# Layer 1 on sums and differences of mirrored tokens, with Fourier weights folded over mirrored channels

## The chip, the cores and the metric

The kernel runs on one core of one Trainium2 chip. The metric is the device time of one execution in microseconds; it is taken from repeated runs, and from one further run that a hardware profiler recorded.

## What is computed

Two layers act on 512 tokens of 2048 features, all in fp32. Cut to what matters here:

```python
for l in range(2):
    shift, scale, gate = split(silu(c) @ w_ada[l] + b_ada[l], 3)
    h = layernorm(x) * (1 + scale) + shift
    u_f, z_f, cq, ckv, k_r, z_a = split(h @ w_in[l])     # 1024, 1024, 512, 256, 64, 1024 columns
    f = real(fft over tokens and over the 128 channels of each of 8 groups of u_f)
    y_f = (f @ w_fmix[l] per group) * silu(z_f)
    y_a = attention(rmsnorm(cq) @ w_q_b, rmsnorm(ckv) @ w_kv_b, k_r) * silu(z_a)
    y = concat(y_f, y_a) @ w_out[l]
    x = layernorm(ALPHA * x + gate * y, ln_g[l], ln_b[l])
```

The real part of a Fourier transform over tokens n and channels m is a sum of cos·cos and −sin·sin products. The cosine in n takes only the sum of the tokens n and 512 − n, the sine only their difference; the same holds for the channels m and 128 − m.

## The kernel before

**Products.** Each fp32 matrix is split into a high part with fewer bits and the rest, and a product is three matmuls (`mm3`, L143 to L146): high·high, high·low, low·high. `split` (L139) makes the parts: ScalarE copies the high one, VectorE subtracts to get the low one. The host sorts the tokens so that n and 512 − n lie in the same row of the blocks 0 and 2, or 1 and 3, of 128 tokens.

**Weights.** `Stream` holds the units of weights in the order of use. A `dense` unit is 256 rows by 512 columns: one DMA from SP's queue into one of three raw buffers (`wr`), one `split`. `st = Stream(4, 2)` loads four units ahead of use and splits two ahead. Converted weights, the activations `h` (16 tiles) and most results share a pool of 35 buffers of 4 KB a partition (`b`). Another pool of nine (`t`) holds short-lived tiles of 512 columns, six buffers (`ada`) take tiles of `w_ada`, and two (`acc`) their running sums. Matmuls write to eight PSUM banks: four `pa` for groups of columns, four `pm` for the rest.

**Order.** The code is unrolled; a planner places each engine's instructions by their place in the text, and may take a later one where an earlier one waits and buffers are free. At run time each engine keeps that order.

**Layer 1.** While the output projection of layer 0 ends row block by row block (L1048), `half_h` (L538) already builds `h` for the tokens of blocks 0 and 1: transposes on TensorE, scale and shift on ScalarE, `split`. `first_group` (L568) takes the first 512 Fourier columns (UA): five units for half of the tokens, then the other half, then `fourier_weights(1)` (two products of fp32 matrices per half of the groups), then three units for all tokens. It is followed by UB, by two groups of Fourier gate columns (ZF), by CQ, CKV and by two groups of attention gate columns (ZA). A group of 512 columns is 8 units of 24 matmuls, each 512 wide. `tm_group` puts tokens on PSUM's partitions, `fm_group` features. `folded` (L627) adds and subtracts the two halves of the tokens of UA and UB, and `fourier` (L597) runs beside the next groups: per block of 128 channels, 14 products with the table over tokens and 6 with the channel table times `w_fmix`. `silu` reads a gate group straight from PSUM; the attention gates wait in DRAM (`szd`).

**Modulation.** `bg_step(n)` (L304) emits n tiles of `w_ada` at a time, each a 512 KB DMA and scaled additions on VectorE (one of 1024 columns per tile for the gates). Layer 1's last 32 tiles, for its output gate, are emitted at 0.7 tiles per unit (`G1`) from UB on, on POOL's DMA queue. `finish` (L245) sums an accumulator over the partitions with transposes and a reduction, adds the bias, and after the last columns writes the gate to DRAM (`gated`). All of it is drained before attention starts.

**Output projection.** Four groups of 512 columns (L1019); for each, the gate's part is read from `gated`, spread over the partitions, into `gb`, and `residual` (L994) multiplies a bank by it and adds it to the scaled input. This frees the bank for the next group.

Of the kernel before, what the change touches and what calls it, by code (L numbers as in the profile page):

```python
# [18 lines left out]
P = 128  # L19
# [4 lines left out]
H = 8  # L24
# [14 lines left out]
class Unit:  # L39
    """One piece of a weight: loaded as it is, then split into a high and a low part."""  # L40
# [15 lines left out]
class Stream:  # L56
    """The weights in the order of their use; next() also starts those that follow."""

    def __init__(self, ahead_raw, ahead):
        self.units, self.ar, self.ac, self.pos = [], ahead_raw, ahead, 0  # L60
        self.limit = None

# [17 lines left out]
def trunk_kernel(ctx: ExitStack, tc: tile.TileContext, x, c, positions, w_ada, b_ada, w_in, q_norm,  # L80
                 w_q_b, kv_norm, w_kv_b, w_fmix, w_out, ln_g, ln_b, dft, chan, invf, odds, out):
    nc = tc.nc
    # layer 0: blocks of 128 features of the input per step, and the part of a step over which the modulation of the
    # next one is spread
    SZ = [1, 2, 3, 4, 6]
    LEADS = [0.5, 0.6, 0.7, 0.5, 0.5]
    # tiles of w_ada per half unit of weights: ahead of need, last step, attention, output projection, layer 1
    ZP, ZL, AP, CP, G1 = 0.5, 1.0, 1.0, 1.4, 0.7
    # half units between the end of a sum over tiles and its sum over the partitions (DL0: in the first step); half
    # units of layer 1 without w_ada tiles  # L90
    DL0, DLY, LATE1 = 2, 3, 4
# [100 lines left out]
    szd = drp.tile([H, P, S], F32, name="szd")  # L192
    gated = drp.tile([DEPTH, D], F32, name="gated")

# [32 lines left out]
    def ada(l, pieces, cols, tiles=None):  # L227
        """One 512 KB tile of w_ada[l] per step; pieces: the column ranges."""
# [38 lines left out]
    def finish_late(steps=None):  # L267
        """Sums over the partitions, some steps after their last term so that TensorE does not wait."""
# [54 lines left out]
    def normalise(t, sums=None):  # L323
        """t: two [128, 1024] tiles, -> (t - mean) * rstd, in place. sums: of the rows of the two tiles, if known."""
# [39 lines left out]
    def dense(src, row0, col0, n, nr=2):  # L364
# [9 lines left out]
        return Unit(load, conv)  # L374
# [52 lines left out]
    for l in range(DEPTH):  # L427
# [7 lines left out]
        else:  # L435
            add_groups(w_in[l], [UA, UB] + ZF + [CQ, CKV] + ZA[:1])
# [10 lines left out]
    def tm_half(banks, w, act, k0, n, first, last, tbs=range(NT)):  # L447
        """token-major: out[tokens, n] += act[k, tokens]^T w[k, n]"""
# [9 lines left out]
    def fm_half(banks, w, act, k0, first, last):  # L458
        """feature-major: out[features, tokens] += w[k, features]^T act[k, tokens]"""
# [9 lines left out]
    def fourier_weights(l):  # L469
# [18 lines left out]
        return cw, dt  # L488

# [48 lines left out]
    def half_h(half, k):  # L538
        """The blocks k, k + 1 of layer 1's features, for half of the tokens."""
        ps = pm()  # L540
        t = t2([P, S])
        ts = slice(half * 256, half * 256 + 256)
        for i in range(2):
            for tb in (2 * half, 2 * half + 1):
                o = i * 256 + (tb % 2) * P
                PE.transpose(out=ps[:, o:o + P], in_=xh[tb][k // 8][:, ((k + i) % 8) * P:][:, :P], identity=ident)  # L546
        for i in range(2):
            m, o = k + i, slice(i * 256, i * 256 + 256)
            if half == 0:
                h[m] = big([P, 2, S])  # L550
            A.activation(t[:, o], ps[:, o], AF.Identity, scale=modT[1][:, 16 + m:17 + m], bias=modT[1][:, m:m + 1])  # L551
            split(h[m][:, 0, ts], h[m][:, 1, ts], t[:, o])
# [3 lines left out]
    for l in range(DEPTH):  # L556
        sums = {}

        def tm_group(g, work=lambda: None):
            banks = [pa() for _ in range(NT)]  # L560
            for k2 in range(8):
                tm_half(banks, st.next(), h, k2 * 2, g[1], k2 == 0, k2 == 7)
                bg_step(G1)
# [4 lines left out]
        def first_group():  # L568
            """The first group of layer 1: half of the tokens starts while the others' layer norm runs."""
            nonlocal cw, dt  # L570
            banks = [pa() for _ in range(NT)]
            for k2 in range(NE):
                tm_half(banks, early[k2], h, k2 * 2, 512, k2 == 0, False, (0, 1))
            for k2 in range(NE, 8):
                half_h(0, k2 * 2)
            for k2 in range(8):
                half_h(1, k2 * 2)
                if k2 < NE:
                    tm_half(banks, early[k2], h, k2 * 2, 512, k2 == 0, False, (2, 3))
            cw, dt = fourier_weights(1)  # L580
# [4 lines left out]
        def fm_group(work=lambda: None):  # L585
            banks = [pa() for _ in range(4)]
            for k2 in range(8):
                fm_half(banks, st.next(), h, k2 * 2, k2 == 0, k2 == 7)
                bg_step(G1)
# [51 lines left out]
        def runner(gen):  # L641
            return lambda: next(gen, None)
# [17 lines left out]
        def latent(src, n, nt):  # L660
            if l == 0:
                p = src
            else:
                t = [big([P, 2, nt], F32) for _ in range(2)]
                p = [t[tb // 2][:, tb % 2] for tb in range(NT)]
                for tb in range(NT):
                    A.copy(p[tb], src[tb][:, :nt])
# [5 lines left out]
            rsqrt_eps(rstd, ssq, 4, 'rms', 1.0 / n)  # L673
            for tb in range(NT):
                V.tensor_scalar(p[tb][:, :n], p[tb][:, :n], rstd[:, tb:tb + 1], None, op0=ALU.mult)
# [10 lines left out]
        def rotary_key(p):  # L686
# [11 lines left out]
            split(kb[:, 0, :, 0], kb[:, 1, :, 0], kr)  # L698
# [166 lines left out]
        if l == 0:  # L865
            # the modulation arrives with the weights: some of the features at a time
# [79 lines left out]
        else:  # L946
            fa = fourier(0, folded(first_group()))
            ub = tm_group(UB, runner(fa))
            drain(fa)
            fb = fourier(1, folded(ub))  # L950
            gate_f(0, silu(fm_group(runner(fb))))
            zs = silu(fm_group(runner(fb)))
            drain(fb)
            gate_f(1, zs)
            lq = latent_q(tm_group(CQ))
            next(lq)
            lkv = latent_kv(tm_group(CKV, runner(lq)))
            next(lkv)
            spill(0, silu(fm_group(runner(lkv))))
            rq = rotary_queries(1)  # L960
            next(rq)
            spill(1, silu(fm_group(runner(rq))))
        project(0)
        drain(rq)
        if l == 1:
            drain(bg)
            finish_late()
# [32 lines left out]
        def finish_rows(tb):  # L1000
# [15 lines left out]
            if l == 0:  # L1016
                normalise(rt[tb], sums if tb < NT - 1 else None)
# [102 lines left out]
```

## Time and profile before

| | us |
|---|---|
| median of three runs (lowest, highest) | 1429.96 (1428.58, 1431.32) |
| profiled execution, first to last instruction | 1430.3 |
| TensorE busy | 1383.3 |
| VectorE busy | 985.8 |
| ScalarE busy | 531.7 |

No time is listed for the profiled execution apart from its span, which is 0.3 us above the median of the runs. A matmul's recorded time includes its way through the array, which overlaps the next one: the distance between starts is what a stream of them costs.

### The profile page before, as it was taken

The page shows a single profiled execution, that of the slowest core. Times are in us where ns is not written, and L with a number is a line of the kernel's source. Part 1 is how long each engine was busy: PE and PEld are TensorE (multiplying, and loading weights), DVE is VectorE, ACT ScalarE, POOL GpSimd, SP SyncE. Part 2 cuts the span into 40 slices and gives each one's busy share as a digit, 9 for nine tenths or more (in the row PEclk, how much of TensorE's full clock was granted, in tenths as well). Part 3 has the DMA queues.
Part 4 walks back from the last instruction along what each step waited for, and adds up shares of the span by engine and source line. Part 5 has one row for each costly group of instructions (what it writes and reads, how often), then busy time and mean ns, then how long its engine had stood idle before and what let it go on. Part 6 is the DMA issues. An engine that isn't in the chain of part 4 may idle for free. (4 is left out here: it accounts for less than half of the span.)

```text
span 1430.3 us, 18410 instructions
## 1 busy us (share of the span) xinstructions
PE 1383.3 (97%) x6941; PEld 1165.0 (81%) x6941; DVE 985.8 (69%) x1598; ACT 531.7 (37%) x931; POOL 50.9 (4%) x77
## 2 busy tenths in 40 slices
PE   4899999999999999999989999999999999999996
PEld 3688888787888888788877888888988888888885
DVE  7799999848968998666689942422325587833448
ACT  6713331224546554212176232422324565522110
POOL 1000000000000000000133100000000000000001
PEclk9999999999999999999999999999999999999999
DMA  8888898824753337876268922520352322272312
GB/s 276 294 286 280 271 348 286 303 74 133 220 192 119 118 104 246 295 253 236 102 234 309 330 71 83 154 70 21 116 148 81 97 59 67 65 252 89 103 60 117
DMA packets 134288, 249.02 MB, mean 174 GB/s; under 512 B 19053, under 2 KB 49913, under 8 KB 134201
## 3 DMA queue, kind: packets, MB, share of 16 engines
q1 hardware_dynamic: 127160, 224.53, 48.4%
q0 software_dynamic: 7040, 23.34, 4.6%
q8 instruction: 54, 0.88, 0.3%
q14 instruction: 34, 0.27, 0.1%
HBM read 235.23 MB, written 12.60 MB: 173 GB/s over the span
## 5 line engine op out<-in xcount | busy, mean ns | idle before, releaser
L144 PE MATMUL pa<-b,b 128*128 128x512 f32 (+2 forms) x1456 | 559.5, 385 | 6.5 <-ACT b L140 5.6
L146 PE MATMUL pa<-b,b 128*128 128x512 f32 (+2 forms) x1456 | 554.8, 382 | 2.3 <-DVE b L141 2.3
L145 PE MATMUL pa<-b,b 128*128 128x512 f32 (+2 forms) x1456 | 555.3, 382 | 0.0
L141 DVE TENSOR_TENSOR b<-wr,b 128x1024 fp32r<-128x1024 f32 (+2 forms) x200 | 228.0, 1148 | 233.2 <-PE pa L145 117.9
L140 ACT CAST b<-wr 128x1024 fp32r<-128x1024 f32 (+2 forms) x200 | 197.7, 998 | 391.5 <-PE pa L146 207.9
L144 PEld LDWEIGHTS pa<-b,b 128*128 128x128 f32 x1456 | 275.0, 189 | 58.8 <-ACT b L140 6.7
L146 PEld LDWEIGHTS pa<-b,b 128*128 128x128 f32 x1456 | 275.1, 189 | 54.2 <-DVE b L141 3.2
L145 PEld LDWEIGHTS pa<-b,b 128*128 128x128 f32 x1456 | 274.9, 189 | 48.7 <-issue 0.7
L240 DVE SCALAR_TENSOR_TENSOR acc<-ada,cact,acc 128x1024 f32<-128x1024 f32 (+2 forms) x193 | 227.7, 1185 | 13.3 <-DMA ada<-in_w_ada_dram 11.3
L144 PE MATMUL pm<-b,b 128*128 128x512 f32 (+3 forms) x592 | 201.7, 343 | 1.8 <-ACT b L140 0.8
L145 PE MATMUL pm<-b,b 128*128 128x512 f32 (+3 forms) x592 | 196.7, 333 | 0.0
L146 PE MATMUL pm<-b,b 128*128 128x512 f32 (+3 forms) x592 | 196.2, 332 | 0.0
L144 PEld LDWEIGHTS pm<-b,b 128*128 128x128 f32 x592 | 111.3, 189 | 19.0 <-ACT b L140 2.7
L145 PEld LDWEIGHTS pm<-b,b 128*128 128x128 f32 x592 | 111.9, 189 | 11.4 <-DVE b L141 0.2
L146 PEld LDWEIGHTS pm<-b,b 128*128 128x128 f32 x592 | 111.8, 189 | 10.5
L140 ACT CAST b<-pm 128x512 fp32r<-128x512 f32 (+1 forms) x116 | 58.1, 533 | 100.3 <-PE pm L605 43.8
L141 DVE TENSOR_TENSOR b<-pm,b 128x512 fp32r<-128x512 f32 (+1 forms) x116 | 68.4, 611 | 34.8 <-ACT b L140 34.7
L140 ACT CAST b<-t 128x512 fp32r<-128x512 f32 (+1 forms) x82 | 41.2, 537 | 53.3 <-DVE t L856 25.6
L900 DVE TENSOR_TENSOR b<-b,pm 128x512 f32<-128x512 f32 (+1 forms) x88 | 55.4, 656 | 5.2 <-PE pm L146 5.0
L141 DVE TENSOR_TENSOR b<-t,b 128x512 fp32r<-128x512 f32 (+1 forms) x82 | 45.2, 576 | 4.0 <-ACT b L140 2.9
L822 ACT ACTIVATE t<-pa,mx 128x512 f32<-128x512 f32 x64 | 43.9, 693 | 10.5 <-DVE mx L819 10.5
L819 DVE TENSOR_REDUCE mx<-pa 128x1 f32<-128x512 f32 x64 | 42.3, 685 | 2.4 <-PE pa L817 2.0
(138 smaller groups left out, 941.8 us busy)
## 6 DMA issues: line engine op xcount, KB each, us to landing
wr<-in_w_in_dram SPq DMA_DIRECT2D x105, 512.0 KB, 4.6
ada<-in_w_ada_dram SPq DMA_DIRECT2D x96, 512.0 KB, 5.5
wr<-in_w_out_dram SPq DMA_DIRECT2D x64, 512.0 KB, 4.1
ada<-in_w_ada_dram SPq DMA_DIRECT2D x96, 256.0 KB, 4.7
ada<-in_w_ada_dram POOLq DMA_DIRECT2D x32, 512.0 KB, 6.1
b<-in_x_dram SPq DMA_DIRECT2D x16, 512.0 KB, 6.5
ada<-in_w_ada_dram SPq DMA_DIRECT2D x32, 192.0 KB, 5.1
wr<-in_w_q_b_dram SPq DMA_DIRECT2D x48, 128.0 KB, 2.9
```

Source lines behind the costliest of these rows:

```text
L140: A.copy(hi, src)
L141: V.tensor_tensor(lo, src, f(hi), op=ALU.subtract)
L144: PE.matmul(o, lh, rh, start=first, stop=False)
L145: PE.matmul(o, lh, rl, start=False, stop=False)
L146: PE.matmul(o, ll, rh, start=False, stop=last)
L240: V.scalar_tensor_tensor(out=a, in0=t[:, r - r0], scalar=cact[:, r:r + 1], in1=a, op0=ALU.mult, op1=ALU.add)
L819: V.reduce_max(mx, ps, axis=AX.X, negate=True)
L822: A.activation(e, ps, AF.Exp, bias=mx, accum_out=ssum)
L900: V.tensor_tensor(s_[tb], s_[tb], banks[tb][:, :n], op=ALU.add)
```

## The change

Layer 1's `h` is built as sums (first 256 columns) and differences (last 256) of mirrored tokens; every projection of layer 1 works on these. The gate groups and the latents add and subtract the halves again after their product (`unfolded`, `latent`), with a factor of one half. All four gate groups now go to DRAM and come back. The Fourier columns are folded over mirrored channels when they are converted: 520 sums (64 per group and the eight middle channels) and 504 differences. The sums of tokens meet only the sums of channels, the differences only the differences (`u_pass`). The tokens 0 and 256, each its own mirror, share a row; its difference over the folded channels is summed on VectorE (`xacc`). Order: ZA0, ZF0, Fourier weights, U, ZF1 (beside the Fourier transform), CQ, CKV, ZA1. The last 32 tiles of `w_ada` are emitted with ZF0, CKV, ZA1 and the first group of the output projection, and are drained after that group.

```diff
-    ZP, ZL, AP, CP, G1 = 0.5, 1.0, 1.0, 1.4, 0.7
+    ZP, ZL, AP, CP, G0, G1 = 0.5, 1.0, 1.0, 1.4, 0.7, 1.2
+    ROWS = [0, 2, 1, 3]
+    FW, UAH = 2, 6
...
+    def fold_unit(src, k):
...
+            w, hi, lo = big([P, 1024], F32), big([P, 1024]), big([P, 1024])
+            c = t.rearrange("p (g c) -> p g c", c=P)
+            e = w[:, 0:512].rearrange("p (g c) -> p g c", c=64)
+            V.tensor_tensor(e[:, :, 1:64], c[:, :, 1:64], c[:, :, 127:64:-1], op=ALU.add)
+            V.tensor_tensor(w[:, 520:1024].rearrange("p (g c) -> p g c", c=63), c[:, :, 1:64], c[:, :, 127:64:-1],
+                            op=ALU.subtract)
+            A.copy(e[:, :, 0], c[:, :, 0])
+            A.copy(w[:, 512:520], c[:, :, 64])
+            split(hi, lo, w)
...
+                V.scalar_tensor_tensor(out=xacc[0][:, :520], in0=w[:, :520], scalar=r, in1=xacc[0][:, :520],
+                                       op0=ALU.mult, op1=ALU.add)
...
+    def pair_h(p, k):
...
+        V.tensor_tensor(v[:, :, 0], t[:, :, 0], t[:, :, 1], op=ALU.add)
+        V.tensor_tensor(v[:, :, 1], t[:, :, 0], t[:, :, 1], op=ALU.subtract)
...
+            def part(w, k0, p, last):
+                wh, wl = w
+                for j in range(4):
+                    js = slice(j * P, (j + 1) * P)
+                    o = banks[j].rearrange("p (x b t) -> p x b t", x=2, b=2)[:, :, p]
...
+                        mm3(o, wh[:, i, js], wl[:, i, js], ah, al, p == 0 and k0 + i == 0, last and i == 1)
+
             for k2 in range(NE):
-                tm_half(banks, early[k2], h, k2 * 2, 512, k2 == 0, False, (0, 1))
+                part(early[k2], k2 * 2, 0, False)
...
             for k2 in range(NE, 8):
-                tm_half(banks, st.next(), h, k2 * 2, 512, False, k2 == 7)
+                fm_half(banks, st.next(), h, k2 * 2, False, k2 == 7)
...
+        def u_pass():
+
+            e, o, b = [pa(), pa()], [pa(), pa()], [pm(), pm()]
+            for k in range(NK):
+                wh, wl = st.next()
+                for p in range(2):
+                    es, os_ = slice(p * P, p * P + P), slice(256 + p * P, 256 + p * P + P)
+                    for bank, ts, cs in ((e[p], es, slice(256, 520)), (b[p], es, slice(0, 256)),
+                                         (o[p], os_, slice(520, 1024))):
+                        mm3(bank[:, :cs.stop - cs.start], h[k][:, 0, ts], h[k][:, 1, ts], wh[:, cs], wl[:, cs],
+                            k == 0, k == NK - 1)
...
+        def fourier_folded(u):
...
+            for b in range(4):
...
+                for i in range(2):
...
+                    mm3(pp[:, 0:258], c[:, 0, gs], c[:, 1, gs], at[:, 0, 0:258], at[:, 1, 0:258], True, False)
+                    mm3(pp[:, 0:258], n[:, 0, gs], n[:, 1, gs], an[:, 0, 0:258], an[:, 1, 0:258], False, True)
+                    mm3(pq[:, 0:256], s_[:, 0, gs], s_[:, 1, gs], at[:, 0, 256:512], at[:, 1, 256:512], True, True)
...
+        def unfolded(banks, dst):
+
+            for j in range(4):
+                t, z = t2([P, S]), t2([P, S])
+                A.copy(t, banks[j])
+                V.tensor_tensor(z[:, 0:256], t[:, 0:256], t[:, 256:512], op=ALU.add)
+                V.tensor_tensor(z[:, 256:512], t[:, 0:256], t[:, 256:512], op=ALU.subtract)
+                A.activation(z, z, AF.Silu, scale=0.5)
+                SP.dma_start(szd[dst + j], z)
...
+            unfolded(first_group(), 0)
+            st.ahead(4, UAH)
+            unfolded(fm_group(ada=G0), H)
+            cw, nq, dt = folded_constants(1)
+            st.ahead(4, 2)
+            fb = fourier_folded(u_pass())
+            unfolded(fm_group(runner(fb, FW)), H + 4)
...
+                if l == 1 and g == 0:
+                    drain(bg)
+                    finish_late()
+                    SP.dma_start(gb, gated[l:l + 1, gs].broadcast_to([P, 512]))
                 for tb in range(NT):
                     residual(g, tb, banks[tb], gb)
```

## Rows read from the trace of the kernel before

**Rows 1.** The page, part 1: busy us (share of the span) and instructions of each engine.

```profile
PE 1383.3 (97%) x6941; PEld 1165.0 (81%) x6941; DVE 985.8 (69%) x1598; ACT 531.7 (37%) x931; POOL 50.9 (4%) x77
```

**Rows 2.** Waits of TensorE, whole span: us in total, times, longest us.

```profile
PE pm L350 <- ACT b L345: 8.9, 4, 2.7
PE pa L144 <- ACT b L140: 5.6, 3, 2.2
```

**Rows 3.** Windows of layer 1: length, busy us of each engine, clock, DMA.

```profile
780.00:800.00 20.00, 20.00 (x92) 16.34 (x91) 19.48 (x26) 9.80 (x17) 5.84 (x11) 1.00 0.96 351
...
820.00:840.00 20.00, 20.00 (x100) 16.71 (x98) 6.20 (x12) 2.92 (x5) 0.00 (x0) 1.00 0.37 122
...
860.00:900.00 40.00, 40.00 (x200) 33.57 (x199) 13.16 (x22) 11.28 (x18) 0.00 (x0) 1.00 0.26 76
```

**Rows 4.** Timeline of TensorE, products 512 wide: start us, us, instruction.

```profile
1147.00 0.39 PE L144 MATMUL pa<-b,b 128*128 128x512 f32 x1
...
1151.76 0.39 PE L144 MATMUL pa<-b,b 128*128 128x512 f32 x1
```

**Rows 5.** Timeline of TensorE, products 256 wide.

```profile
1141.50 0.28 PE L145 MATMUL pa<-b,b 128*128 128x256 f32 x1
...
1144.13 0.28 PE L146 MATMUL pa<-b,b 128*128 128x256 f32 x1
```

**Rows 6.** Timeline of TensorE: a Fourier block of 14 products, and what follows.

```profile
798.22 0.28 PE L144 MATMUL pm<-b,b 128*128 128x258 f32 x1
...
800.27 0.39 PE L146 MATMUL pa<-b,b 128*128 128x512 f32 x1
```

**Rows 7.** Timeline of TensorE: the fp32 products of the Fourier weights, and what follows.

```profile
776.07 3.05 PE L478 MATMUL pm<-b,b 128*128 128x512 f32 x6
778.56 0.80 PE L144 MATMUL pa<-b,b 128*128 128x512 f32 x1
```

**Rows 8.** The page, part 5: out<-in xcount | busy, mean ns | idle before.

```profile
L144 PEld LDWEIGHTS pa<-b,b 128*128 128x128 f32 x1456 | 275.0, 189 | 58.8 <-ACT b L140 6.7
```

**Rows 9.** Groups of VectorE by line and shape.

```profile
L141 DVE TENSOR_TENSOR b<-wr,b 128x1024 fp32r<-128x1024 f32 x169 | 205.5, 1223 | 187.8 <-PE pa L145 109.1 <-ACT b L140 50.9 <-issue 14.8
...
L240 DVE SCALAR_TENSOR_TENSOR acc<-ada,cact,acc 128x1024 f32<-128x1024 f32 x150 | 192.4, 1283 | 5.4 <-DMA ada<-in_w_ada_dram 3.6
...
L240 DVE SCALAR_TENSOR_TENSOR acc<-ada,cact,acc 128x512 f32<-128x512 f32 x28 | 20.2, 751 | 3.5 <-DMA ada<-in_w_ada_dram 3.3
...
L141 DVE TENSOR_TENSOR b<-t,b 128x256 fp32r<-128x256 f32 x34 | 13.0, 418 | 0.7 <-PE pm L681 0.5 <-ACT b L140 0.2
...
L634 DVE TENSOR_TENSOR t<-pa,t 128x512 f32<-128x512 f32 x6 | 4.1, 684 | 0.6 <-ACT t L633 0.6
```

**Rows 10.** Windows at the border of the layers.

```profile
737.40:741.00 3.60, 3.59 (x9) 2.87 (x10) 3.14 (x6) 3.60 (x8) 2.57 (x3) 0.54 1.00 312
...
751.00:754.50 3.50, 2.03 (x9) 0.84 (x7) 3.50 (x6) 3.50 (x10) 0.73 (x1) 0.98 1.04 414
754.50:758.00 3.50, 3.50 (x9) 2.59 (x10) 3.04 (x12) 2.09 (x4) 0.66 (x1) 0.53 0.60 221
...
758.00:763.00 5.00, 5.00 (x33) 4.29 (x32) 4.78 (x8) 4.62 (x11) 1.63 (x3) 1.00 0.55 165
```

**Rows 11.** Timeline, all engines: from the sums of the last gate columns to their store.

```profile
1116.71 1.03 PE L253 MATMUL pm<-ident,acc 128*128 128x128 f32 x8
...
1119.57 0.33 SPq L262 DMA_DIRECT2D gated<-t  x1
```

**Rows 12.** DMA issues: count, KB each, median us to landing.

```profile
t<-gated SPq DMA_DIRECT2D x8, 256.0 KB, 4.6
...
gated<-t SPq DMA_DIRECT2D x2, 8.0 KB, 3.0
```

**Rows 13.** Timeline of VectorE: the residual of a group in the output projection.

```profile
1284.09 0.70 DVE L996 TENSOR_TENSOR pa<-pa,t 128x512 f32<-128x512 f32 x1 [0.30 <-PE pa L146]
1284.83 0.69 DVE L997 SCALAR_TENSOR_TENSOR b<-b,pa 128x512 f32<-128x512 f32 x1
```

More of the change, by code (lines that the diff above doesn't have):

```diff
@@ L61, in __init__, with ahead @@
         self.limit = None
+    def ahead(self, raw, conv):
+        self.ar, self.ac = raw, conv
     def add(self, u):
@@ L435, in trunk_kernel @@
         else:
[L436 removed]
+            add_groups(w_in[l], [ZA[0], ZF[0]])
+            for k in range(NK):
+                st.add(fold_unit(w_in[l], k))
+            add_groups(w_in[l], [ZF[1], CQ, CKV])
             for k2 in range(8):
@@ L488, in fourier_weights, with folded_constants, keep @@
         return cw, dt
+    def folded_constants(l):
+        def keep(shape, dt=F32R):
+            n[0] += 1
+            if n[0] <= 6:
+                return adp.tile(shape, dt, tag="ada", name=nm("fc"))
+            return big(shape, dt)
+        n = [0]
+        cw, nq, dt = [[None, None], [None, None]], [], []
+        cc = big([P, 2, P], F32)
+        GP.dma_start(cc, chan.rearrange("a p c -> p a c"))
+        wf = big([P, G, P], F32)
+        SP.dma_start(wf, w_fmix[l].rearrange("g m d -> m g d"))
+        for hf in range(2):
+            for a in range(3):
+                lhs = big([P, P], F32)
+                if a < 2:
+                    for d in range(2):
+                        V.tensor_copy(lhs[:, d * 64:d * 64 + 64], cc[:, a, 0:64])
+                else:
+                    V.tensor_copy(lhs, cc[:, 0, 64:65].broadcast_to([P, P]))
+                ps = pm()
+                PE.matmul(ps, lhs, wf[:, hf * 4:hf * 4 + 4].rearrange("p g d -> p (g d)"), start=True, stop=True)
+                t = keep([P, 2, 512])
+                if a < 2:
+                    V.memset(f(t), 0.0)
+                    for d in range(2):
+                        rs = slice(d * 64, d * 64 + 64)
+                        o, i = (x.rearrange("p (g e c) -> p g e c", e=2, c=P)[:, :, d] for x in (t[rs, 0], ps[rs]))
+                        A.copy(o, i)
+                        V.tensor_tensor(t[rs, 1].rearrange("p (g e c) -> p g e c", e=2, c=P)[:, :, d], i, f(o),
+                                        op=ALU.subtract)
+                    cw[a][hf] = t
+                else:
+                    for g in range(4):
+                        cs, m = slice(g * P, g * P + P), ident[:, 120 + hf * 4 + g:121 + hf * 4 + g]
+                        scaled(t[:, 0, cs], t[:, 1, cs], ps[:, cs], m)
+                    nq.append(t)
+        for k in range(2):
+            t = keep([P, 2, S])
+            for a in range(2):
+                GP.dma_start(t[:, a], dft[a, k * P:(k + 1) * P, :])
+            dt.append(t)
+        return cw, nq, dt
     def rotary_tables():
@@ L557, in trunk_kernel, with tm_group @@
         sums = {}
-        def tm_group(g, work=lambda: None):
+        def tm_group(g, work=lambda: None, ada=0):
             banks = [pa() for _ in range(NT)]
@@ new lines, in gates @@
+        def gates():
+            for j in range(8):
+                sz = t2([P, S])
+                SP.dma_start(sz, szd[H + j])
+                yj = yf[j // 2][:, j % 2]
+                V.tensor_tensor(yj, yj, sz, op=ALU.mult)
+                yield
+        def unfolded(banks, dst):
[6 more added lines that the diff above has]
+                SP.dma_start(szd[dst + j], z)
@@ L644, in drain, with runner, run @@
+        def runner(gen, n=1):
+            def run():
+                for _ in range(n):
+                    next(gen, None)
+            return run
         def drain(gen):
@@ L664, in latent @@
                 t = [big([P, 2, nt], F32) for _ in range(2)]
-                p = [t[tb // 2][:, tb % 2] for tb in range(NT)]
-                for tb in range(NT):
-                    A.copy(p[tb], src[tb][:, :nt])
+                p = [t[tb % 2][:, tb // 2] for tb in range(NT)]
+                for tb in range(2):
+                    b = t2([P, S])
+                    A.copy(b[:, :nt], src[tb + 2][:, :nt])
+                    V.tensor_tensor(p[tb], src[tb][:, :nt], b[:, :nt], op=ALU.add)
+                    V.tensor_tensor(p[tb + 2], src[tb][:, :nt], b[:, :nt], op=ALU.subtract)
+            half = 0.5 if l else 1.0
             ssq = sm(4, 'ssq')
@@ L697, in rotary_key @@
             kb = big([P, 2, NT, 2, 64])
-            split(kb[:, 0, :, 0], kb[:, 1, :, 0], kr)
+            if l == 0:
+                split(kb[:, 0, :, 0], kb[:, 1, :, 0], kr)
+            else:
+                scaled(kb[:, 0, :, 0], kb[:, 1, :, 0], kr, 0.5)
             for a in range(2):
@@ L1016, in finish_rows @@
             if l == 0:
-                normalise(rt[tb], sums if tb < NT - 1 else None)
+                normalise(rt[tb], sums if tb != ROWS[-1] else None)
         for g in range(4):
@@ L1048, in trunk_kernel @@
                         SP.dma_start(lgb[i][j], src[l:l + 1, j * 1024:(j + 1) * 1024].broadcast_to([P, 1024]))
-                for tb in range(NT):
+                for tb in ROWS if l == 0 else range(NT):
                     ts = slice(tb * P, (tb + 1) * P)
@@ L1056, in trunk_kernel @@
                     finish_rows(tb)
-                    if l == 0 and tb == HA:
+                    if l == 0 and tb == ROWS[HA]:
                         xh = rt
```

163 lines of the change are left out of this document (120 added, 43 removed).

## The prediction, made before the changed kernel ran

> **What bounds the kernel now.** I read the page's first part, the waits of TensorE, the windows of layer 1 and then the timeline of each place that the change touches. TensorE is busy in 1383.3 of 1430.3 us, VectorE in 985.8, ScalarE in 531.7 [rows 1]. After the first loads the waits of TensorE are few: 8.9 us where the first rows are normalised, 5.6 us on weights or activations from ScalarE, none longer than 2.7 us [rows 2]. So a TensorE product that goes away shortens the run, unless what fed it beside comes late. In layer 1's windows TensorE is busy throughout, while VectorE goes from 19.5 of 20 us at 780 to 800 (it runs ahead with the tiles of w_ada there) down to 6.2 of 20 and 13.2 of 40 later [rows 3]. The border of the layers is the one weak place: at 751 to 754.5 TensorE is busy 2.0 of 3.5 us, and in the next 3.5 us the granted clock is 0.53, its 1.2 GHz level [rows 10].
>
> **The price of a product.** From start to start: 21 products 512 wide from 1147.00 to 1151.76 are 0.227 us each [rows 4]; 22 products 256 wide from 1141.50 to 1144.13 are 0.120 us each [rows 5]. The cost follows the width, and the weight load (189 ns recorded [rows 8]) hides even behind 0.120 us.
>
> **TensorE's sum.** (a) U before: two groups of 8 units of 24 products, 384 × 0.227 = 87.1 us. After: 16 units, each 2 halves × 3 banks × 3 products of 264, 256 and 504 columns, so 96 × (0.120 + 0.120 + 0.223) = 44.4 us (0.223 is 504/512 of 0.227). Saved: 42.6 us. (b) Fourier: a block of 14 products took from 798.22 to 800.27, 2.05 us [rows 6]; six more at 0.120 make 2.77, and there are 8: 22.2 us. After: one block of 8 products, 2.05 − 6 × 0.120 = 1.33 us; four blocks of 14, 8.2 us; eight times 9 products, 72 × 0.120 = 8.6 us; together 18.2. Saved: 4.0 us. (c) The fp32 products of the Fourier weights: 6 records from 776.07 to 778.56 are 0.415 us each, and a product has two [rows 7]. Two more products cost 1.7 us. (d) `part`: 5 units × 2 halves × 24 products 256 wide, 28.8 us, for 120 products 512 wide, 27.2 us: 1.6 us more. These products write two runs of 128 columns of a bank, which no row shows; I take 0.120 us, and the other end is that of a full-width product, 0.227, which adds 25.7 us. (e) Four products for the row sums: 0.5 us. Sum: −42.6 − 4.0 + 1.7 + 1.6 + 0.5 = −42.8 us.
>
> The Trainium skill, "SBUF — State Buffer", section "Door 1: The DMA port swizzle", says that a PSUM pattern that is not contiguous slows matmuls down a good deal; here only the jump between two contiguous runs is of that kind, and no row shows one.
>
> **The border of the layers.** Before, all 8 units had products for the first half of the tokens: 96 × 0.227 = 21.8 us of work while the last row block was normalised. After, units 5 to 7 take both halves at once, so only 5 × 24 × 0.120 = 14.4 us stand there: 7.4 us of cover is gone. `pair_h` puts an addition and a subtraction of 256 columns (0.418 us each [rows 9]) into the chain of the second half: 0.8 us. Both are on the path, as nothing else is ready for TensorE: 8.2 us. The ends: 3 us if the hole that exists at 751 absorbs the rest; 14 us if the 5 early pairs' additions on VectorE (5 × 0.84 us, with VectorE busy 4.78 of 5 us there) delay the last row too, and the clock falls once more for 1.7 us, as 3.6 us at 0.54 lose 46% [rows 10]).
>
> **Feeding the U pass.** A folded unit costs VectorE an addition and a subtraction of 504 (0.684 each, by the row of 512), the split's 1.223 and a scaled addition of 520 (0.751): 3.34 us [rows 9], 16 × 3.34 = 53.5 us, where TensorE needs 2.8 us a unit. The constants add about 9 us of VectorE (copies, clears, 8 subtractions of 256 at 0.418 and 8 of 128). What hides this is the gate group before, 43.5 us long, in which VectorE had some 27 of 40 us free [rows 3], as six units may be split ahead. With six ready, 10 × 3.34 + 9 = 42.4 us lie beside 46.7 (44.4, plus 5.1 for six fp32 products, less the last unit): nothing. With four ready 49.1: 2.4 us. With none 62.5: 15.8 us. I take four, 2.4 us, as the buffers `b` also hold 16 tiles of h and the constants; ends 0 and 16. That step −1 along the channels costs VectorE no more than step 1 is assumed; no row shows it.
>
> **Costed at nothing.** The additions and subtractions of `unfolded` and of the latents (about 20 us of VectorE in four groups), eight more stores and loads of 256 KB on SP's queue and the copies on ScalarE lie beside groups of 43.5 us in which VectorE was busy a third [rows 3]; a bank is copied before the group's end needs it. Without that cover each of six changes of group could wait the 0.6 us of a copy and 0.7 of a sum: I put 1 us in all, up to 8. The tiles of w_ada that move cost the same 32 × 1.283 us [rows 9] and lie beside the same stage.
>
> **The gate of the output projection.** A new wait. The last tile is emitted in the sixth unit of the first group, and its sum over the partitions only after the group's last product. From these transposes to the store of the gate took 1116.71 to 1119.57, 2.9 us [rows 11]; the store lands in 3.0 us, the spread-out load in 4.6 [rows 12]; the residual's two operations on a bank take 0.70 and 0.69 [rows 13]. Until then all four `pa` banks are full, and no later work of TensorE is ready: 11.9 us. Behind the wait on VectorE stand the residuals and the splits from the third unit of the next group on, on SP the loads of later weights; both have units ready. A pause of this kind was followed by 3.6 us at a clock of 0.54 [rows 10], 1.7 us lost. Together 13.5 us. Ends: 0, if the planner puts the transposes earlier into a gap of TensorE (the running sum will be complete long before), and 16.
>
> **Sum.** −42.8 + 8.2 + 2.4 + 1 + 13.5 = −17.7 us on the profiled span of 1430.3, which is 0.3 us above the median of the runs: 1412.6, against the median 1412 us.
>
> **The rivals.**
> 1. The gate's wait is hidden. For: VectorE did the w_ada tiles early in windows 780 to 820, so the planner moves work up. Against: this sum's transposes came no earlier than their place in the text although VectorE was idle well before [rows 11, 3]. 1412 − 13.5 = 1399 us.
> 2. VectorE bounds the U pass, with no unit ready and the gate's wait too. For: 3.34 us against 2.8 a unit. Against: the free time in the gate group. 1412 + 13.4 = 1425 us.
> 3. The other side: the folded units can't run ahead at all, because a unit wants three buffers of `b` at once and the pool is full; then split and products of a unit take turns, 3.34 + 2.8 = 6.1 us, 16 × 6.1 − 44.4 − 2.4 = 51 us more: 1463 us. It decides from 3.9 us a unit on (2.8 + 17.7/16), where the gain is gone. For: splits already wait mostly for TensorE to free buffers (109.1 of 187.8 us idle [rows 9]). Against: 35 less 16 for h and 2 for the table leaves room for five or six.
> 4. The split PSUM writes of `part` at full price: 1412 + 25.7 = 1438 us.
> 5. Half the width does not halve the time, if each product costs at least its weight load of 0.189 us [rows 8]: U after is then 96 × (0.189 + 0.189 + 0.223) = 57.7 us, 13.3 more: 1425 us. Rows 5 speak against it.
>
> The Trainium skill, "TensorE: Matmul & The Clock Gate", section "Back-to-back issue gap", says that in a stream of loads and products both set the spacing, with about 131 ns at 512 columns and 81 ns at 128; by it (98 ns at 256, my estimate from these two) the U pass would save 384 × 0.131 − 96 × 0.327 = 19 us instead of 42.6. This trace has 227 and 120 ns instead, so I give that rule little.
>
> **Chances.** Forecast 0.47 (its own range 1404 to 1420), rival 1 0.25, rival 2 0.12, rival 3 (with milder forms from 1433 on) 0.10, rival 4 0.04, rival 5 0.02. A difference under 0.2%, 2.9 us, can't be told from none. Faster: 0.47 + 0.25 + two thirds of rivals 2 and 5, 0.09, so 0.81. Same: the other third and the mildest of rival 3, 0.06. Slower: 0.13. The range 1396 to 1430 leaves out rivals 3 and 4 and a little on the low side, where gate and border both cost less.
>
> **What would show it.** In the profile after: 96 products each of 264, 256 and 504 columns; starts 0.12 us apart at 256, in `part` too (else rival 4); TensorE's wait on VectorE or ScalarE inside the U pass near 2 us (over 13 us: rival 2 or 3); one pause of about 12 us at the end of the output projection's first group, followed by a clock near 0.5 (none: rival 1); about 8 us more of holes and low clock at the border. A VectorE operation along the reversed channels well over 0.68 us would break the feed, and the forecast with it.

## The result, and the profile after

The changed kernel takes 1414.27 us (median of four runs, 1412.58 to 1416.38) against 1430.32 (four runs): a ratio of 0.9891, 95% interval 0.9876 to 0.9905. The forecast was 1412, range 1396 to 1430. The profiled execution spans 1414.6 us, 15.7 less than that of before.

The page of the changed kernel, part 1, against [rows 1]: busy us (share of the span) and instructions of each engine.

```profile
PE 1348.8 (95%) x6949; PEld 1145.5 (81%) x6949; DVE 1041.5 (74%) x1739; ACT 541.3 (38%) x988; POOL 50.9 (4%) x77
```

TensorE is busy 34.5 us less, VectorE 55.7 us more. Busy time mixes speeds, so I also summed the products of each trace, by width, each at the distance between starts at full clock (0.227 us at 512 columns, 0.223 at 504, 0.122 at 264, 0.120 at 256, and so on), and took the sum from the span. What is left over is loss: idle time and low clock. Before: 1358.7 us of work and 71.6 of loss. After: 1316.2 and 98.4. So 42.5 us of work went and 26.8 us of loss came; the prices of the few odd widths move either figure by some 1 us. Where the loss came is in the waits.

Waits of TensorE in the changed kernel, whole span, against [rows 2]: us in total, times, longest us.

```profile
PE pm L355 <- ACT b L350: 8.5, 4, 2.7
PE pa L149 <- DVE b L1218: 8.0, 1, 8.0
PE pm L632 <- ACT b L350: 7.7, 2, 6.6
PE pa L149 <- ACT b L145: 5.7, 5, 1.8
PE pm L632 <- ACT t L636: 2.4, 3, 1.6
PE pm L264 <- DVE modT L219: 1.8, 1, 1.8
```

The first and the fourth row stood there before. New are one pause of 8.0 us in the output projection (L1218 is the residual that frees a bank) with 1.8 us for the transpose of the gate's columns just ahead of it, and the pause of 6.6 us at the border of the layers.

Groups of TensorE in the U pass of the changed kernel (840 to 900 us), one row for each width: instructions | busy us, mean ns. Beside them the stream's own distances, from the timeline.

```profile
L149 PE MATMUL pa<-b,b 128*128 128x504 f32 x32 | 12.5, 390 | 0.0
...
L149 PE MATMUL pa<-b,b 128*128 128x264 f32 x32 | 9.5, 296 | 0.0
...
L149 PE MATMUL pm<-b,b 128*128 128x256 f32 x32 | 8.9, 279 | 0.0
```

```profile
851.83 0.28 PE L149 MATMUL pa<-b,b 128*128 128x264 f32 x1
...
852.20 0.39 PE L149 MATMUL pa<-b,b 128*128 128x504 f32 x1
...
852.88 0.28 PE L149 MATMUL pa<-b,b 128*128 128x264 f32 x1
```

There are 32 products of each width on each of three lines, 96 as predicted. Three products lie between one of these starts and the next: 0.12 us each at 264 columns and 0.227 at 504, where the prediction had 0.223 (0.4 us in all). `part`, which writes two runs of 128 columns of a bank, streams at the same 0.12 us per 256 columns:

```profile
743.02 0.28 PE L150 MATMUL pa<-b,b 128*128 128x256 f32 x1
...
744.46 0.28 PE L150 MATMUL pa<-b,b 128*128 128x256 f32 x1
```

Twelve products lie between these two starts, 1.44 us. That ends rivals 4 and 5.

The Trainium skill, "SBUF — State Buffer", section "Door 1: The DMA port swizzle", would have slowed a PSUM pattern that is not contiguous; the trace doesn't show that for two runs of 128 columns. The spacing that the Trainium skill's "TensorE: Matmul & The Clock Gate" gives under "Back-to-back issue gap" for 512 columns (131 ns) is again not met: 227 ns at 504.

The gate: timeline of the changed kernel, TensorE and SP's issues, against [rows 11]: start us, us, instruction [idle before <- releaser].

```profile
1262.34 0.27 PE L264 MATMUL pm<-ident,modT 128*16 128x128 f32 x1 [1.76 <-DVE modT L219]
1270.57 0.76 PE L149 MATMUL pa<-b,b 128*128 128x512 f32 x1 [7.95 <-DVE b L1218]
1271.13 0.63 PE L150 MATMUL pa<-b,b 128*128 128x512 f32 x1
1271.56 0.63 PE L151 MATMUL pa<-b,b 128*128 128x512 f32 x1
```

```profile
1262.93 0.33 SPq L267 DMA_DIRECT2D gated<-t  x1
1265.06 0.35 SPq L1259 DMA_DIRECT2D t<-gated  x1
```

The gate is stored at 1262.93, read back from 1265.06, and the first product of the next group starts at 1270.57; the following products are 0.43 us apart, the lower clock level. From 1255 to 1285 the loss is 11.3 us.

The border: VectorE in the changed kernel, from the last row block's mean and variance (`out_mv`, L320) to the next step of its norm (`out_v`, L186).

```profile
737.12 0.26 DVE L320 BATCH_NORM_AGGREGATE out_mv<-bns 128x2 f32<-128x24 f32 x1
737.29 1.23 DVE L245 SCALAR_TENSOR_TENSOR acc<-ada,cact,acc 128x1024 f32<-128x1024 f32 x1
738.45 1.22 DVE L146 TENSOR_TENSOR b<-wr,b 128x1024 fp32r<-128x1024 f32 x1
...
740.25 0.42 DVE L638 TENSOR_TENSOR t<-t 128x256 f32<-128x256 f32 x1
...
747.12 1.23 DVE L146 TENSOR_TENSOR b<-wr,b 128x1024 fp32r<-128x1024 f32 x1 [2.17 <-ACT b L145]
748.26 0.42 DVE L639 TENSOR_TENSOR t<-t 128x256 f32<-128x256 f32 x1
748.60 0.15 DVE L186 TENSOR_SCALAR out_v<-out_mv 128x1 f32<-128x1 f32 x1
```

And the same two steps in the kernel before:

```profile
736.25 0.26 DVE L315 BATCH_NORM_AGGREGATE out_mv<-bns 128x2 f32<-128x24 f32 x1
...
737.02 0.15 DVE L181 TENSOR_SCALAR out_v<-out_mv 128x1 f32<-128x1 f32 x1
```

What was 0.8 us is 11.5: the norm's next step, 0.15 us long, stands behind four splits of weights, the pairs' additions and splits, and a wait of 2.17 us for a unit of weights. The norm as a whole is far less late than this step. Its last operation on ScalarE, in the changed kernel and in the kernel before:

```profile
760.47 2.37 ACT L350 ACTIVATE b<-b,nmr,ln_rstd 128x1024 f32<-128x1024 f32 x2 [1.12 <-DVE nmr L348]
```

```profile
756.42 2.38 ACT L345 ACTIVATE b<-b,nmr,ln_rstd 128x1024 f32<-128x1024 f32 x2 [1.41 <-DVE nmr L343]
```

It ends 25.7 us after that mean and variance, before 22.6: 3.2 us later. In between TensorE starts 97 products of 256 columns, 11.6 us of work, before 62 of 512 columns, 14.1 us; VectorE is busy 23.1 of the 25.7 us.

From 720 to 800 us the loss is 22.6 us, before 10.9: 11.7 us more. Windows of this stretch and of the 10 us behind the norm's end, the changed kernel first, then the kernel before (length, busy us of PE, PEld, DVE, ACT, POOL, clock, DMA):

```profile
720.00:800.00 80.00, 66.44 (x398) 59.30 (x397) 66.55 (x128) 54.03 (x106) 10.63 (x14) 0.87 0.52 170
...
762.85:772.85 10.00, 7.89 (x39) 6.90 (x38) 9.52 (x21) 9.29 (x23) 0.00 (x0) 0.54 0.19 54
```

```profile
720.00:800.00 80.00, 74.61 (x334) 58.31 (x333) 73.18 (x114) 52.54 (x101) 25.36 (x42) 0.96 0.84 297
...
758.80:768.80 10.00, 10.00 (x55) 8.46 (x53) 9.81 (x16) 7.72 (x20) 3.22 (x6) 1.00 0.84 268
```

TensorE is idle 13.6 us there, before 5.4: 8.2 of the 11.7 us. The other 3.5 us are low clock, the most of it behind the pause of 6.6 us, where the granted clock is 0.54 and before was 1.00.

### The profile page after: what moved, and what is told of

Read it like the earlier page. It is cut to its first block, busy times and chain, and to the rows that moved or that the text cites. A ratio compares the mean times of both kernels' runs of the same rounds, so it can differ in the third digit from the quotient of the medians.

```text
span 1414.6 us, 18714 instructions
## 1 busy us (share of the span) xinstructions
PE 1348.8 (95%) x6949; PEld 1145.5 (81%) x6949; DVE 1041.5 (74%) x1739; ACT 541.3 (38%) x988; POOL 50.9 (4%) x77
## 5 line engine op out<-in xcount | busy, mean ns | idle before, releaser
L149 PE MATMUL pa<-b,b 128*128 128x512 f32 (+4 forms) x1432 | 538.0, 377 | 15.3 <-DVE b L1218 8.0
L150 PE MATMUL pa<-b,b 128*128 128x512 f32 (+4 forms) x1432 | 535.6, 374 | 1.0 <-DVE b L146 1.0
L151 PE MATMUL pa<-b,b 128*128 128x512 f32 (+4 forms) x1432 | 533.9, 374 | 0.7 <-DVE b L146 0.6
L146 DVE TENSOR_TENSOR b<-wr,b 128x1024 fp32r<-128x1024 f32 (+3 forms) x184 | 208.4, 1141 | 155.5 <-PE pa L150 92.0
L149 PEld LDWEIGHTS pa<-b,b 128*128 128x128 f32 x1432 | 271.7, 190 | 62.5 <-issue 8.4
L145 ACT CAST b<-wr 128x1024 fp32r<-128x1024 f32 (+3 forms) x184 | 180.2, 989 | 365.2 <-PE pa L151 189.2
L151 PEld LDWEIGHTS pa<-b,b 128*128 128x128 f32 x1432 | 271.6, 190 | 47.3 <-DVE b L146 1.7
L150 PEld LDWEIGHTS pa<-b,b 128*128 128x128 f32 x1432 | 272.1, 190 | 45.4 <-DVE b L146 1.8
L145 ACT CAST b<-pm 128x512 fp32r<-128x512 f32 (+4 forms) x110 | 54.9, 529 | 81.2 <-PE pm L797 17.8
L146 DVE TENSOR_TENSOR b<-pm,b 128x512 fp32r<-128x512 f32 (+4 forms) x110 | 64.6, 609 | 18.5 <-ACT b L145 18.4
L145 ACT CAST b<-t 128x512 fp32r<-128x512 f32 (+1 forms) x73 | 35.8, 524 | 49.8 <-DVE t L1073 25.6
L146 DVE TENSOR_TENSOR b<-t,b 128x512 fp32r<-128x512 f32 (+1 forms) x73 | 39.4, 565 | 4.5 <-ACT b L145 4.0
```

Source lines behind the costliest of these rows:

```text
L145: A.copy(hi, src)
L146: V.tensor_tensor(lo, src, f(hi), op=ALU.subtract)
L149: PE.matmul(o, lh, rh, start=first, stop=False)
L150: PE.matmul(o, lh, rl, start=False, stop=False)
L151: PE.matmul(o, ll, rh, start=False, stop=last)
```

## The experiments

All times are medians; the kernel before took 1430.73 us beside the first four kernels, 1430.61 beside the next four and 1431.9 beside the last four, so a difference of medians is good to some 2 us here: taken from the ratios, the differences below come out up to 1.7 us otherwise.

**The gate's sum back before the attention.** `drain(bg)` and `finish_late()` stand ahead of the attention again, and the first group's `gb` is loaded like the others.

```diff
+        if l == 1:
+            drain(bg)
+            finish_late()
...
-            if l == 0 or g > 0:
+            if True:
...
-                if l == 1 and g == 0:
-                    drain(bg)
-                    finish_late()
-                    SP.dma_start(gb, gated[l:l + 1, gs].broadcast_to([P, 512]))
```

> The last tiles of w_ada and their sum over the partitions are emitted before attention again, as in the kernel before; the rest is the changed kernel. Theory (the gate's wait is a pause of TensorE that nothing covers): the pause at the end of the output projection's first group (8.0 us for the residual and 1.8 us for the sum, then a low clock; 11.3 us lost in that stretch by price of products) goes, 1414.3 - 11 = 1403 us. Rival (the tiles cost as much where they go, since VectorE and the DMA queues are needed there): the pause goes but as much is lost earlier, 1411 to 1416 us.

1402.54 us (1402.01 to 1403.04), ratio 0.9801 (0.9786 to 0.9815): 11.7 us less than the change (12.9 by the ratios), and faster than both kernels. The window of the output projection, this kernel first, then the changed one (length, busy us of PE, PEld, DVE, ACT, POOL, clock, DMA):

```profile
1240.00:1290.00 50.00, 50.00 (x223) 41.40 (x222) 17.10 (x20) 9.51 (x9) 0.00 (x0) 1.00 0.37 111
```

```profile
1240.00:1290.00 50.00, 40.28 (x175) 32.99 (x175) 16.04 (x22) 7.64 (x8) 0.00 (x0) 0.90 0.33 102
```

The pause and the low clock behind it are gone, and nothing takes their place.

**The wait alone, in the kernel before.** The late sum put into the kernel before, with `G1` lowered so that tiles are left for the first group.

```diff
-    ZP, ZL, AP, CP, G1 = 0.5, 1.0, 1.0, 1.4, 0.7
+    ZP, ZL, AP, CP, G1 = 0.5, 1.0, 1.0, 1.4, 0.45
...
-        if l == 1:
-            drain(bg)
-            finish_late()
...
+                if l == 1 and g == 0:
+                    drain(bg)
+                    finish_late()
+                    SP.dma_start(gb, gated[l:l + 1, gs].broadcast_to([P, 512]))
```

> The kernel before with one part of the change alone: the last tiles of w_ada are spread up to the first group of the output projection (0.45 tiles a unit) and drained only after it, and the gate's first load comes after that. Theory: the wait alone costs 11 us, 1430.3 + 11 = 1441 us, with a pause of TensorE near 8 us on the residual. Rival (in this kernel the planner finds a gap for the sum, so the price belongs to the changed order): 1430 us.

1443.02 us, ratio 1.0082 (1.0067 to 1.0097): 12.3 us more. Its waits of TensorE:

```profile
PE pa L144 <- DVE b L994: 7.7, 1, 7.7
...
PE pm L259 <- DVE modT L214: 1.8, 1, 1.8
```

They are the changed kernel's, 7.7 for 8.0 and 1.8 for 1.8. Taken away the wait gives 11.7 us, added it costs 12.3 (11.7 by the ratio): it stands by itself.

**The lost cover given back.** Units 5 to 7 of the first group also go through `part`, so that all eight have products for the first half of the tokens.

```diff
+                early.append(st.next())
+                part(early[k2], k2 * 2, 0, False)
             for k2 in range(8):
                 pair_h(1, k2 * 2)
-                if k2 < NE:
-                    part(early[k2], k2 * 2, 1, False)
-            for k2 in range(NE, 8):
-                fm_half(banks, st.next(), h, k2 * 2, False, k2 == 7)
+                part(early[k2], k2 * 2, 1, k2 == 7)
```

> Units 5 to 7 of layer 1's first group are again taken in two halves, the first tokens' half before the second half of h is built; 72 products 512 wide become 144 of 256 (1 us more by price). Theory (the border lost 11.6 us more than before because 7.4 us of products no longer cover the last row's norm, plus a longer low clock): the idle 6.6 us before the last row's transposes shrinks to about nothing, 1414.3 - 8 = 1406 us, at most 1403. Rival (the hole comes from VectorE's additions in the build of h, which delay the last row): the products just move, 1412 to 1415 us.

1414.01 us, ratio 0.9878 (0.9862 to 0.9895): no gain to be told from nothing. The theory, which was the prediction's, fell. The step from `out_mv` to `out_v` takes 11.4 us here too, and TensorE's wait has only changed its place: it now stands at a pair that comes out of VectorE's queue behind the norm (5.4 us).

```profile
735.00 0.26 DVE L320 BATCH_NORM_AGGREGATE out_mv<-bns 128x2 f32<-128x24 f32 x1
...
746.43 0.15 DVE L186 TENSOR_SCALAR out_v<-out_mv 128x1 f32<-128x1 f32 x1
```

```profile
PE pa L149 <- ACT b L145: 10.7, 6, 5.4
```

The edit moves 72 products ahead, yet from the last mean and variance to the norm's end, again 25.7 us, TensorE starts only 12 more than in the changed kernel, 109 instead of 97. So the cover was offered, but little of it was ready in time: the pairs that it needs come out of the same queue as the norm.

**Both together.**

> The last tiles of w_ada emitted before attention, and units 5 to 7 of the first group taken in halves, both on the changed kernel. Theory (two separate pauses): the gains add, 1414.3 - 11 - 8 = 1395 us. Rival (w_ada's tiles and the build of h need the same engine at the same time): less than the sum of the two, 1400 us or more.

1404.5 us (1399.52 to 1407.18), ratio 0.9811 (0.9788 to 0.9834): the gate's gain and nothing beside it.

**Without the additions.** `pair_h` hands its rows on as they are; sums and differences of the tokens are left out.

```diff
-        V.tensor_tensor(v[:, :, 0], t[:, :, 0], t[:, :, 1], op=ALU.add)
-        V.tensor_tensor(v[:, :, 1], t[:, :, 0], t[:, :, 1], op=ALU.subtract)
+        v = t
```

> The changed kernel without the addition and the subtraction that make sums and differences of the pairs of h (it leaves these out; everything after uses the rows as they are). Theory: what the border of the layers lost is VectorE's queue, in which each of the 8 pairs now stands twice, so that the last row's norm and the last pairs' hand-over come late; without the additions the border gives back 7 to 9 us: 1406 us. Rival, the products that no longer cover the norm: their number is the same here, so only the 0.8 us of the last pair's additions goes: 1413 us.

1407.1 us, ratio 0.9844 (0.9832 to 0.9857): 7.2 us less than the change, as the theory of VectorE's queue had it. From 720 to 800 us the loss falls from 22.6 to 14.9, and the norm's step no longer waits:

```profile
730.71 0.26 DVE L320 BATCH_NORM_AGGREGATE out_mv<-bns 128x2 f32<-128x24 f32 x1
...
734.16 0.14 DVE L186 TENSOR_SCALAR out_v<-out_mv 128x1 f32<-128x1 f32 x1
```

3.45 us instead of 11.5; the norm's end comes 23.8 us after the mean and variance instead of 25.7, and TensorE is idle 8.6 us from 720 to 800 instead of 13.6. The edit frees VectorE of 32 operations, takes 0.8 us out of each pair's way from its transposes to its products, and lets the planner place the norm's step earlier; these can't be told apart by it.

**Without the additions, and the cover back.**

> As the run before (no additions), and units 5 to 7 also split into halves, so that all 8 units have products for the first half of the tokens. Theory: the cover counts only while VectorE isn't the one that is late; with its queue free some of it comes back, 2 to 6 us under the run without additions: 1400 to 1404 us. If the last row's norm still ends after both, the products only move and the time is that of the run without additions, within 1.5 us.

1407.24 us, ratio 0.9846 (0.9832 to 0.9861): no less than without the cover. The 2 to 6 us of the theory didn't come. TensorE's waits from 720 to 800 us say why; the run without the cover first, then this one:

```profile
PE pm L632 <- ACT b L350: 3.8, 2, 2.7
```

```profile
PE pa L150 <- DVE b L146: 1.6, 1, 1.6
...
PE pm L632 <- ACT b L350: 1.1, 1, 1.1
```

With less in VectorE's queue, only 3.8 us of waiting for the norm were left to cover. The cover takes 2.7 of them, and 1.6 come back as waits for splits. The border's loss is 1.8 us smaller in the trace (13.1); the times can't tell that from nothing.

**A slower fold.** The fold's first addition done three times, 1.35 us more of VectorE a unit.

```diff
-            V.tensor_tensor(e[:, :, 1:64], c[:, :, 1:64], c[:, :, 127:64:-1], op=ALU.add)
+            for _ in range(3):
+                V.tensor_tensor(e[:, :, 1:64], c[:, :, 1:64], c[:, :, 127:64:-1], op=ALU.add)
```

> The changed kernel with the first addition of a folded unit done three times, 1.35 us more of VectorE a unit, 21.6 us in all; the output stays the same. Theory: the U pass was fed with slack, as six units run ahead and VectorE has free time in the gate group before it: at most 2 us more, 1414 to 1416 us. Rival: the feed is on its edge (4.7 us a unit against TensorE's 2.8), and the units that are not ready ahead make TensorE wait: 12 to 20 us more, 1426 to 1434 us.

1429.33 us (12 runs), ratio 0.9991 (0.9978 to 1.0003): 15 us more; my theory of slack fell, the rival holds. TensorE's timeline in its U pass, where a unit starts:

```profile
881.37 0.39 PE L149 MATMUL pa<-b,b 128*128 128x264 f32 x1 [1.04 <-ACT b L145]
886.26 0.39 PE L149 MATMUL pa<-b,b 128*128 128x264 f32 x1 [1.50 <-ACT b L145]
891.18 0.39 PE L149 MATMUL pa<-b,b 128*128 128x264 f32 x1 [1.52 <-ACT b L145]
```

A unit every 4.9 us, about the fold's own time (3.34 + 1.35), where TensorE needs 2.8; from 880 to 900 us the granted clock is 0.91, where it was 1.00. Six units were folded before the pass here as in the change. The ten that are left take 49 us, and the prediction's 9 us of constants stand beside them, against 47 us of TensorE; my expectation had forgotten that the free time before the pass holds six units and no more.

**Two units ahead instead of six.**

```diff
-    FW, UAH = 2, 6
+    FW, UAH = 2, 2
```

> The changed kernel with two folded units split ahead of the U pass instead of six. Theory: four more units must be made inside the pass, 4 x 3.3 us of VectorE; it then has 14 x 3.3 + 9 = 55 us of work beside 46.7 us of TensorE: 8 us more, 1422 us. Rival: the order in which the work is planned brings the units forward into VectorE's free time all the same, and nothing changes: 1414 us.

1421.74 us, ratio 0.994 (0.9924 to 0.9956): 7.5 us more, against 8 expected. The loss from 850 to 950 us is 7.3 us, in the change 0.6. The match is partly luck. The planner does bring two units forward: four, not two, are split before the pass's first product (the fourth split starts at 841.03, the product at 843.52), in the change six. And in the pass a unit takes 3.6 us, not 3.3: that far apart its splits start, in the change too, as each waits for ScalarE's part.

**Every product of the U pass twice** (U comes out doubled).

```diff
-                        mm3(bank[:, :cs.stop - cs.start], h[k][:, 0, ts], h[k][:, 1, ts], wh[:, cs], wl[:, cs],
-                            k == 0, k == NK - 1)
+                        for again in range(2):
+                            mm3(bank[:, :cs.stop - cs.start], h[k][:, 0, ts], h[k][:, 1, ts], wh[:, cs], wl[:, cs],
+                                k == 0 and again == 0, k == NK - 1 and again == 1)
```

> The changed kernel with every product of the U pass done twice (U comes out doubled; all else the same). Theory: the U pass is bound by TensorE and a product costs its width, also at 256 and 264 columns: 96 x (0.120 + 0.122 + 0.223) = 44.6 us more, less what the folded units, which then have more time to be made, no longer hold up (under 1 us): 1458 to 1459 us. Rival: half-width products cost more than their width when they come in a row (0.189 us, the weight load): 96 x (0.189 + 0.189 + 0.223) = 57.7 us more, 1472 us. Second rival: part of the pass's time is waiting for VectorE, which the added products hide: under 1450 us.

1461.67 us, ratio 1.0219 (1.0199 to 1.0239): 47.4 us above the change by the medians, 43.4 by the profiled spans (1458.0 and 1414.6). The 44.6 of the theory lies between; neither 57.7 nor less than 36 does. The pass in this run:

```profile
850.00:950.00 100.00, 100.00 (x629) 89.98 (x628) 45.53 (x75) 24.80 (x57) 0.00 (x0) 1.00 0.26 77
```

TensorE is busy throughout at full clock: half-width products in a row cost about half, 0.12 us against 0.227.

**The additions on GpSimd,** in three kernels that all have the gate's sum early (1402.54 us, ratio 0.9801, is what they are to beat): those of the first half, the subtraction of both halves, and all.

```diff
-        V.tensor_tensor(v[:, :, 0], t[:, :, 0], t[:, :, 1], op=ALU.add)
-        V.tensor_tensor(v[:, :, 1], t[:, :, 0], t[:, :, 1], op=ALU.subtract)
+        (GP if p == 0 else V).tensor_tensor(v[:, :, 0], t[:, :, 0], t[:, :, 1], op=ALU.add)
+        (GP if p == 0 else V).tensor_tensor(v[:, :, 1], t[:, :, 0], t[:, :, 1], op=ALU.subtract)
```

> The kernel with the gate's sum back before the attention, and the additions and subtractions of the first-half pairs on GpSimd instead of VectorE (the same output). Theory: what the border lost is VectorE's queue ahead of the last row's norm; 8 x 0.84 us leave it, so 3 to 6 us under the 1402.5 us of the kernel with the gate alone: 1397 to 1400 us, if an operation of 256 columns takes GpSimd about 0.65 us (twice the 0.319 us of its one row of 128 columns). Rival: GpSimd is several times slower or holds VectorE up, and the pairs come later than before: 1404 us or more.

> As the run before, but only the subtraction of each pair on GpSimd, in both halves, beside the addition on VectorE (the same output). Theory: 0.42 us leaves VectorE's queue in each of 16 pairs, half of it ahead of the last row's norm: 2 to 4 us under 1402.5, 1398 to 1400 us. Rival, GpSimd slow: each pair then waits for it in its chain, 16 x 0.5 us or more in the second half alone: 1404 us or more.

> Both operations of both halves on GpSimd, with the gate's sum back before the attention (the same output). Theory: VectorE is free of 13.4 us, as in the run without additions, which gave 7 us: 1396 to 1398 us. Rival: in the second half the pairs are a chain from TensorE to TensorE, and two operations in a row on GpSimd make each link longer, so that it loses there what it wins before the norm: 1402 us or more.

1409.02 us (ratio 0.9843, 0.9827 to 0.9859), 1411.87 (0.9868, 0.9848 to 0.9889) and 1414.23 (0.9877, 0.9861 to 0.9894): all slower than without, by 0.0042 to 0.0076 of 1430 us, 6 to 11 us. All three theories fell. From the first of them, GpSimd's groups over the whole span:

```profile
L639 POOL TENSOR_TENSOR t<-t 128x256 f32<-128x256 f32 x8 | 9.1, 1137 | 0.0
L638 POOL TENSOR_TENSOR t<-t 128x256 f32<-128x256 f32 x8 | 8.1, 1015 | 4.1 <-ACT t L636 3.9
```

and VectorE's splits of weights from 735 to 755 us, in this run and in the change:

```profile
L146 DVE TENSOR_TENSOR b<-wr,b 128x1024 fp32r<-128x1024 f32 x6 | 8.8, 1481 | 0.0
```

```profile
L146 DVE TENSOR_TENSOR b<-wr,b 128x1024 fp32r<-128x1024 f32 x6 | 7.3, 1222 | 2.2 <-ACT b L145 2.2
```

An addition takes GpSimd 1.02 to 1.14 us on average instead of VectorE's 0.42, and the splits that run beside it take VectorE 1.48 instead of 1.22. What was taken off VectorE's queue came back as longer operations: from the last mean and variance to the norm's end VectorE is busy 28.6 us, in the kernel with the gate alone 23.1. The loss from 720 to 800 us is 25.5 us, with the additions on VectorE 22.3. In this run the norm's next step comes 6.2 us after the mean and variance instead of 11.1 in that kernel, and still the norm ends after 31.8 us instead of 25.4: that short step does not decide when the norm is done.

The Trainium skill has this beforehand, in "SBUF — State Buffer", section "🔬 SBUF: two separate sides": VectorE's operations with two inputs from SBUF and GpSimd's that read SBUF shut each other out of a shared pair of ports for a whole instruction. The stretched splits have two inputs from SBUF and agree with it.

## Why the prediction was right

**TensorE's sum** (−42.8 predicted): −42.5 by the products, good to some 1 us. Doubling the pass's products, 43.4 to 47.4 us for 44.6, shows that this is what they cost.

**The gate's wait** (13.5): 11.3 by the loss in the trace, 11.7 by its removal, 12.3 by its addition. The pause began where predicted and the clock fell behind it as predicted; it was some 2 us shorter. Rival 1 is out.

**The border** (8.2, up to 14): 11.7, so mis-sized by 3.5 us, and in the main for the wrong reason. That TensorE's idle time grew by just 8.2 us is luck; the 3.5 us more are low clock behind the pause, which the step had only in its upper end, with 1.7. The step had put 7.4 us on products that no longer cover the last row's norm, 14.4 us of them instead of 21.8. In the traces 11.6 and 14.1 us are started between that row's mean and variance and its norm's end, 2.4 us apart, and offering the cover again gained nothing. Taking the additions away gave 7.2 us. So it is VectorE's queue that decides, with the norm, the pairs and the splits in it: the norm ends 3.2 us later, and pairs come late with it. That stood in the prediction only as the upper end. How much is the additions' own time and how much the order that the planner chose is open, and so are the 4 us of the 11.7 that stay without the additions: up to 1.8 of them may be the cover, and no run tells the rest apart.

**The feed of the U pass** (2.4): 0.6 of loss from 850 to 950 us. Six units were ready where I had taken four (the sixth split starts at 830.28, the pass's first product at 848.53); the bound worked out for six, nothing, is what came. The bounds were real: 1.35 us a unit more costs 15 us, and two instead of six ahead cost 7.5. With four ready the step's 2.4 us would have been too little: the run that had four lost 7.3, at 3.6 us a unit instead of 3.34. So rivals 2 and 3 did not come, by a small margin. The reversed step costs nothing: the fold's two operations, with one input read backwards, took 677 and 674 ns at 504 columns against 684 at 512 [rows 9].

```profile
L397 DVE TENSOR_TENSOR b<-wr 128x504 f32<-128x504 f32 x16 | 10.8, 677 | 0.0
L396 DVE TENSOR_TENSOR b<-wr 128x504 f32<-128x504 f32 x16 | 10.8, 674 | 0.1
```

**Costed at nothing** (1): from 950 to 1010 us the loss is 3.1 us, before 0.4 from 900 to 1000, so some 2.5: two waits for the copy of a gate's bank, 0.9 and 0.6 us (L842), and 0.9 us in which the transposes of the latents wait for VectorE (L889).

Together −42.5 + 11.7 + 11.3 + 0.6 + 2.5 = −16.4, against −15.7 by the spans. The mechanisms of TensorE's sum and of the gate were right. That the sum came within 2.3 us of the time is luck beyond that: the gate and the feed were put too high, the border and the terms costed at nothing too low.

## What to carry to other kernels

A saving of TensorE's work is worth the number of products times their spacing at that width, if the feed holds: count what VectorE needs a unit against TensorE, with the units ready beforehand, and try how thin the margin is, since two fifths more work in the fold (1.35 us on 3.34) took the whole gain. When a stage's start gets later, follow the whole chain that makes it ready in both traces: here one step of it came 10.7 us later and its end only 3.2. And count cover by the products that were ready in time, not by those that the code offers; add the low clock that followed the pause. Last, keep a reduction that goes through DRAM away from the place where all banks are full: moved ahead of the attention it cost nothing that a run shows, and this version, 1402.5 us, has the lowest median of all.

## What was not expected of the hardware

An idle GpSimd was not free: in the first of the three runs its additions of 256 columns took 0.72 to 1.75 us, and VectorE's operations that ran with them grew (the norm's two of 1024 columns from 1.28 to 1.52 us on average). And neither a PSUM bank written in two runs (0.12 us for 256 columns) nor an input read backwards (0.677 and 0.674 us for 504 columns) cost anything.
